# Sixty-four tokens by row instead of fifty-six, selected first with a row for each token and head, in the expert layer of a hybrid decoder step

## The chip, the cores and the metric

One core of one Trainium2 chip runs the whole program. The metric is the device time of one execution in microseconds (us); the time before is 2587.82 us, the median of three runs (2585.52 to 2590.06).

## The reference, cut to what matters

The program is one decoder layer for 264 tokens (256 of a prompt and 8 samples) of width 2048 in float32. The change touches one part of it, the PEER expert layer: each token gets 8 heads of queries, each query is scored against two sets of 128 keys, the 16 best of each set are combined to 256 candidates, and the 16 best candidates name 16 of 16384 experts. An expert is one row of `u_tab` and one row of `v_tab`.

```python
def peer(x, w_q, keys1, keys2, u_tab, v_tab):
    q = (xt @ w_q).reshape(n_pad, PEER_HEADS, 2, PEER_DKEY // 2)
    s1 = jnp.einsum('thd,hkd->thk', q[:, :, 0], keys1)
    s2 = jnp.einsum('thd,hkd->thk', q[:, :, 1], keys2)
    t1, i1 = lax.top_k(s1, PEER_TOPK)
    t2, i2 = lax.top_k(s2, PEER_TOPK)
    cand = (t1[..., :, None] + t2[..., None, :]).reshape(n_pad, PEER_HEADS, PEER_TOPK * PEER_TOPK)
    cand_idx = (i1[..., :, None] * PEER_KEYS + i2[..., None, :]).reshape(...)
    top, pos = lax.top_k(cand, PEER_TOPK)
    idx = jnp.take_along_axis(cand_idx, pos, axis=-1)
    gate = jax.nn.softmax(top, axis=-1)
    hid = jax.nn.gelu(jnp.einsum('td,thkd->thk', xb, u_tab[ib]), approximate=False)
    coef = gb * hid
    return jnp.einsum('thk,thkd->td', coef, v_tab[ib])
```

## The kernel before, in words

**Precision.** Every dense product is split: a weight tile of 128 x 1024 is loaded from DRAM by the SP queue (L142), ScalarE casts it to its high part (L153) and VectorE subtracts to get the low part (L154). Such a tile is half of a block of 128 output columns, a "half-block". Five tiles can wait for the split and four, later five, can be split ahead of the matmuls.

**The experts, two ways.** For most tokens (`TD = T - NSP`, 208 before) all 16384 experts are computed densely. In the U stage, 128 blocks (`pair_block`, L263) multiply x1 by the whole of `u_tab`; the activations go to DRAM (`a_d`). Meanwhile `gates` builds for each token a 128 x 128 map of its gates from one-hot operands (three of four on POOL, the fourth on VectorE, the others on ScalarE, a matmul each) and writes it to DRAM (`g_d`). In the V stage, 8 times 16 blocks multiply activations times gates (`prep`, L1408) by `v_tab` and add into `acc` (L1454). A block has 16 matmuls over 2 x TD columns (L273, L276: the weights' high part against both parts of the tokens) and 16 over TD columns (L274: the low part).

For the last `NSP` tokens (56 before: 48 of the prompt and the 8 samples) the experts' rows are gathered instead (`sparse_experts`, L1261). A gather of 128 rows of 8 KB by row numbers in `sidx` (L1269, on POOL's queue) fills a tile `ug`, and VectorE either multiplies and sums it against the tokens' own x1 (L1339, for `u`) or adds it times a coefficient to `x1s` (L1347, L1349, for `v`). The tokens come in groups of 32, 16 and 8 (`GR`); at a group's end matmuls with `fld` fold the 128 rows back to the tokens (L1310). A gathered tile needs 1 MB; there are 56 for `u` and 56 for `v`.

**The selection.** The scores of all tokens are computed head by head during the query product before U (`head_topk`, L1074): two tiles of 128 tokens with a column for each head, and one in which the 8 samples have a row for each sample and head. `topk` takes five VectorE operations for 16 of 128. `select` (L1110) then works in the U stage, on the second 128 tokens, the samples, and the first 128 tokens, in that order: 16 of 112 candidates per head, then a lookup of the two key numbers in three passes over 16 x 16 (compare with an iota, multiply, sum: L1161, L1164, L1166). `send` (L1210) writes row numbers and gates of the rowwise tokens to DRAM, and `index` (L1273) loads them back with a row for each token and slot. Three transposes (L1196) bring the selection of the dense tokens to `slot`, from which `gates` reads.

**The order.** It is written out by the program. After each half-block `tick(budget)` lets background tasks issue instructions: each task says after a piece how much VectorE time it thinks to have used (`yield 1.1`), or that it waits some half-blocks (`yield ("w", 2)`). The budget of a half-block is 1.1 in U and V. A gathered tile is due each 3.5 half-blocks until `to_v` and each 3.75 after it (L1336); `gates` puts four tokens in each 3 half-blocks. V can start when the gates are done ("G0") and `prep(0)` has run. On every engine the instructions run in the order in which they were issued.

Of the kernel before, what the change touches and what calls it, by code (L numbers as in the profile page):

```python
# [17 lines left out]
D = 2048  # L18
# [4 lines left out]
NSP = 56  # L23
# [24 lines left out]
GR = ((0, 32), (32, 16), (48, 8))  # L48
# [3 lines left out]
def hybrid_step(ctx: ExitStack, tc: tile.TileContext, xT, pT, w_in, w_dt, w_bs, w_bc, w_o, w_q, w_pg, w_pp,  # L52
# [64 lines left out]
    fld = cpool.tile([128, NSP], F, name="fld")  # L117
    x1sp = cpool.tile([128, KB, NSP], F, name="x1sp")
    sidx = cpool.tile([128, NSP], U32, name="sidx")
    scf = cpool.tile([128, NSP], F, name="scf")  # L120
    shid = cpool.tile([128, NSP], F, name="shid")
# [906 lines left out]
    keys_sb = {}  # L1028
    Q = {}

    TT = ((PT // 2, 128, PH), (PT, 64, 1), (0, 128, PH))
# [8 lines left out]
    TV = [[t1.tile([128, nh, TOPK], F, name=f"tv{t}{s}") for s in range(2)] for t, (_, _, nh) in enumerate(TT)]  # L1040
    TI = [[t1.tile([128, nh, TOPK], U32, name=f"ti{t}{s}") for s in range(2)] for t, (_, _, nh) in enumerate(TT)]
    zq = t2.tile([128, 2, PH, 64], F, name="zq")
    gp.memset(zq, 0.0)
    SC, P = {}, {}
# [4 lines left out]
    def load_keys(h):  # L1049
        k = t2.tile([128, 2, 128], F, name="keys", tag="keys", bufs=2)  # L1050
        gp.dma_start(out=k, in_=keysT[:, 2 * h:2 * h + 2, :])
        keys_sb[h] = k

    def q_evac(j):
        def f(ps):
            def late():
                t, sb = n1.product(ps)
                soon(lambda: ac.activation(t, t, AF.Identity, bias=sb))
                Q[j] = t
                if j % 2 == 1:  # L1060
                    spawn(head_topk(j // 2))

            defer(3, late)
        return f

    def topk(v, a, i, n):
        ve.max(a[:, 0:8], v)
        ve.max_index(i[:, 0:8], a[:, 0:8], v)
        w = t2.tile([128, 128], F, name="sw", tag="sw", bufs=2)
# [4 lines left out]
    def head_topk(h):  # L1074
        load_keys(h)
        yield ("w", 2)
        for s in range(2):
            ac.copy(zq[:, s, h, 8 * h:8 * h + 8], Q[2 * h + s][:, PT:T])
        yield ("w", 1)
        k = keys_sb.pop(h)  # L1080
        ps2 = {}
        for t in (0, 2):
            t0, n, _ = TT[t]
            ps = bank("scr")
            for s in range(2):
                te.matmul(ps[:n, s * 128:(s + 1) * 128], Q[2 * h + s][:, t0:t0 + n], k[:, s], start=True, stop=True)
            v = t2.tile([128, 2, 128], F, name="sv", tag="sv", bufs=3)
            ac.copy(v[:n].rearrange("p s k -> p (s k)"), ps[:n, 0:256])  # L1088
            ps2[t] = v
            yield 0.1  # L1090
        if h == 0:
            SC["ps"] = bank("scp")
        for s in range(2):
            te.matmul(SC["ps"][:64, s * 128:(s + 1) * 128], zq[:, s, h], k[:, s],
                      start=(h == 0 and s == 0), stop=(h == PH - 1), skip_group_check=True)
        if h == PH - 1:
            v = t2.tile([128, 2, 128], F, name="sv", tag="sv", bufs=3)
            ac.copy(v[:64].rearrange("p s k -> p (s k)"), SC.pop("ps")[:64, 0:256])
            ps2[1] = v
        for t, v in sorted(ps2.items()):  # L1100
            n = TT[t][1]
            for s in range(2):
                hh = h if t != 1 else 0
                topk(v[:n, s], TV[t][s][:n, hh], TI[t][s][:n, hh], n)
                yield 1.1
        Q.pop(2 * h)
        Q.pop(2 * h + 1)
        DONE[h] = True

    def select(t, sel):  # L1110

        _, n, nh = TT[t]
        sp = P["sp"]
        w = nh * TOPK
        top = sp.tile([128, nh, TOPK], F, name="top", tag="top", bufs=1)
        pos_u = sp.tile([128, nh, TOPK], U32, name="posu", tag="posu", bufs=1)

        cand = sp.tile([128, nh, 112], F, name="cand", tag="cand", bufs=1)
        v1, v2 = TV[t][0][:n], TV[t][1][:n]
        ve.tensor_tensor(cand[:n, :, 0:64].rearrange("p h (a b) -> p h a b", b=16),  # L1120
                         v1[:, :, 0:4, None].to_broadcast([n, nh, 4, 16]),
                         v2[:, :, None, :].to_broadcast([n, nh, 4, 16]), OP.add)
        ve.tensor_tensor(cand[:n, :, 64:112].rearrange("p h (a b) -> p h a b", b=4),
                         v1[:, :, 4:16, None].to_broadcast([n, nh, 12, 4]),
                         v2[:, :, None, 0:4].to_broadcast([n, nh, 12, 4]), OP.add)
        yield 1.1
        for h in range(nh):
            cf = cand[:n, h]
            a, i = top[:n, h], pos_u[:n, h]
            ve.max(a[:, 0:8], cf)  # L1130
            ve.max_index(i[:, 0:8], a[:, 0:8], cf)
            ve.match_replace(cf, a[:, 0:8], cf, NEG)
            ve.max(a[:, 8:16], cf)
            ve.max_index(i[:, 8:16], a[:, 8:16], cf)
            yield 0.95
        pu = pos_u[:n].rearrange("p h k -> p (h k)")
        ab_f = sp.tile([128, 4, w], F, name="abf", tag="abf", bufs=1)
        sh = sp.tile([128, w], U32, name="sh", tag="sh", bufs=2)
        ve.tensor_scalar(sh[:n], pu, 4, None, OP.logical_shift_right)
        ve.tensor_copy(ab_f[:n, 2], sh[:n])  # L1140
        sh = sp.tile([128, w], U32, name="sh", tag="sh", bufs=2)
        ve.tensor_scalar(sh[:n], pu, 2, None, OP.logical_shift_right)
        ve.tensor_copy(ab_f[:n, 3], sh[:n])
        fa, fb = ab_f[:n, 0], ab_f[:n, 1]
        ve.scalar_tensor_tensor(fa, ab_f[:n, 3], -12.0, ab_f[:n, 2], OP.add, OP.max)
        ve.tensor_scalar(ab_f[:n, 2], fa, 4.0, 48.0, OP.mult, OP.add)
        ve.scalar_tensor_tensor(ab_f[:n, 2], fa, 16.0, ab_f[:n, 2], OP.mult, OP.min)
        ve.tensor_copy(fb, pu)
        ve.tensor_tensor(fb, fb, ab_f[:n, 2], OP.subtract)
        yield 1.4  # L1150
        HH = max(1, nh // 4)
        for s in range(2):
            af = ab_f[:, s].rearrange("p (h k) -> p h k", h=nh)
            idf = sp.tile([128, nh, TOPK], F, name="idf", tag="idf", bufs=1)
            ve.tensor_copy(idf[:n], TI[t][s][:n])
            sv = sel[:n, s].rearrange("p (h k) -> p h k", h=nh)
            for h0_ in range(0, nh, HH):
                hs = slice(h0_, h0_ + HH)
                big = sp.tile([128, HH, TOPK, TOPK], F, name="big", tag="big", bufs=1)
                sh4 = [n, HH, TOPK, TOPK]  # L1160
                ve.tensor_tensor(big[:n], af[:n, hs, :, None].to_broadcast(sh4),  # L1161
                                 iot[:n, None, None, 0:TOPK].to_broadcast(sh4), OP.is_equal)
                yield 0.6 if nh > 1 else 0.4
                ve.tensor_tensor(big[:n], big[:n], idf[:n, hs, None, :].to_broadcast(sh4), OP.mult)  # L1164
                yield 0.6 if nh > 1 else 0.4
                ve.tensor_reduce(sv[:, hs], big[:n], AX.X, OP.add)  # L1166
                yield 0.6 if nh > 1 else 0.4
        gt = sel[:n, 2].rearrange("p (h k) -> p h k", h=nh)
        ve.tensor_tensor(gt, top[:n], top[:n, :, 0:1].to_broadcast([n, nh, TOPK]), OP.subtract)
        yield ("w", 1)  # L1170
        ac.activation(gt, gt, AF.Exp)
        sm = sp.tile([128, nh], F, name="sm", tag="sm", bufs=2)
        ve.tensor_reduce(sm[:n], gt, AX.X, OP.add)
        ve.reciprocal(sm[:n], sm[:n])
        ve.tensor_tensor(gt, gt, sm[:n, :, None].to_broadcast([n, nh, TOPK]), OP.mult)
        yield 0.8

    def select_all():
        while sum(h in DONE for h in range(PH)) < PH:
            yield ("w", 1)  # L1180
        t2_stack.close()
        sp = P["sp"] = sp_stack.enter_context(tc.tile_pool(name="select", bufs=1))
        P["oh"] = oh_stack.enter_context(tc.tile_pool(name="onehot", bufs=1))
        for t, (t0, n, nh) in enumerate(TT):
            sel = sp.tile([128, 3, nh * TOPK], F, name=f"sel{t}")
            yield from select(t, sel)
            if t < 2:
                send(sel, t, nh)
            if t == 1:
                spawn(sparse_experts(), True)  # L1190
            if t != 1:
                nd = min(n, TD - t0)
                yield ("w", 2)
                ps = bank("slt")
                for q in range(3):
                    te.transpose(ps[:, q * 128:q * 128 + n], sel[:n, q], ident[:n, :n])  # L1196
                for q in range(3):
                    ac.copy(slot[q][:, t0:t0 + nd], ps[:, q * 128:q * 128 + nd])
                if t == 0:
# [467 lines left out]
```

## Time and profile before

| | |
|---|---|
| three runs | 2585.52, 2587.82, 2590.06 us |
| the profiled execution | 2587.27 us, of which the span is 2585.5 us |
| granted TensorE clock, mean | 0.998 |
| bytes moved by DMA | 689.02 MB, mean 266 GB/s |
| the query product with the key scores | about 1020 to 1142 us |
| U stage | 1142.1 to 1829.9 us |
| V stage | 1829.9 to 2466 us |

A profile shows one execution. PE is TensorE, PEld its weight loads, DVE VectorE, ACT ScalarE, POOL GpSimd, SP the queue that loads weights. The recorded length of a matmul includes its way through the array, and neighbours overlap, so the distance between two starts tells what a matmul costs. A share of busy time is a mean over the whole span.

### The profile page before, as it was taken

What the parts mean: (1) busy time and instruction counts of PE and PEld (TensorE: products, weight loads), DVE (VectorE), ACT (ScalarE), POOL (GpSimd) and SP (SyncE); (2) the same over time, 40 slices, a digit from 0 to 9 for tenths busy, and PEclk for the clock granted to TensorE, in tenths of its full rate; (3) what the DMA queues carried; (4) which work ended last, traced back from release to release, by engine and by line L of the source; (5) the groups of instructions that cost most, each with busy time, mean ns of one, the idle gap of its engine ahead of it and who ended that gap; (6) DMA issues with size and microseconds to landing.
All of it is one profiled execution on the core that took longest, in us unless ns stands there. A gap on an engine that the chain in (4) does not pass through costs nothing.

```text
span 2585.5 us, 49226 instructions
## 1 busy us (share of the span) xinstructions
PE 2556.8 (99%) x19049; PEld 2532.4 (98%) x19049; DVE 2038.0 (79%) x3296; ACT 1433.7 (55%) x2206; POOL 620.6 (24%) x720
## 2 busy tenths in 40 slices
PE   9999999999999999999999999999999999999999
PEld 9999999999999999999999999999999999999999
DVE  7899965557445557889989777778889988889986
ACT  5665543445334444655578778866544454444563
POOL 2332200000000010100148567633332223222210
PEclk9999999999999999999999999999999999999999
DMA  6798765655665655567779999999999999999664
GB/s 229 228 292 282 244 184 168 183 175 181 180 184 178 183 179 180 172 186 221 220 243 365 363 357 357 356 364 376 375 362 377 371 364 356 375 358 366 206 196 123
DMA packets 202779, 689.02 MB, mean 266 GB/s; under 512 B 23040, under 2 KB 60464, under 8 KB 187312
## 3 DMA queue, kind: packets, MB, share of 16 engines
q1 hardware_dynamic: 154832, 495.49, 57.9%
q0 software_dynamic: 28688, 158.69, 16.1%
q10 hardware_dynamic: 19024, 31.69, 3.3%
q8 instruction: 149, 2.44, 0.4%
q14 instruction: 86, 0.70, 0.1%
HBM read 646.32 MB, written 39.46 MB: 265 GB/s over the span
## 4 chain that ended last, share of the span: by engine, by line
PE 72%; DVE 14%; DMA 9%; issue 3%; ACT 2%; ACTq 0%; POOL 0%; SPq 0%; DVEq 0%; POOLq 0%
PE mm L273 17%; PE mm L239 14%; PE mm L237 14%; PE mm L238 14%; PE mm L274 9%; DVE wlo L154 6%; DMA w<-vP 5%; DMA w<-uT 2%; PE gps L1258 1%; ACT whi L153 1%; PE mm L276 1%; DVE ug L1339 1%; DMA w<-w_in 1%; DVE as L1384 1%; DVE x1s L1349 1%
## 5 line engine op out<-in xcount | busy, mean ns | idle before, releaser
L154 DVE TENSOR_TENSOR wlo<-w,whi 128x1024 fp32r<-128x1024 f32 x916 | 1114.5, 1223 | 412.3 <-ACT whi L153 409.6
L153 ACT CAST whi<-w 128x1024 fp32r<-128x1024 f32 x916 | 958.5, 1050 | 754.3 <-PE mm L238 283.9
L273 PE MATMUL mm<-x,whi 128*128 128x416 f32 x1920 | 593.0, 370 | 0.0
L273 PE MATMUL mm<-co,whi 128*128 128x416 f32 x1920 | 586.6, 367 | 0.0
L239 PE MATMUL mm<-x,wlo 128*128 128x264 f32 x1920 | 547.9, 285 | 4.1 <-DVE wlo L154 4.0
L237 PE MATMUL mm<-x,whi 128*128 128x264 f32 x1920 | 546.8, 285 | 0.0
L238 PE MATMUL mm<-x,whi 128*128 128x264 f32 x1920 | 544.8, 284 | 0.0
L274 PE MATMUL mm<-x,wlo 128*128 128x208 f32 x2048 | 510.6, 259 | 5.7 <-DVE wlo L154 5.2
L274 PE MATMUL mm<-co,wlo 128*128 128x208 f32 x2048 | 510.4, 259 | 2.8 <-DVE wlo L154 2.6
L274 PEld LDWEIGHTS mm<-x,wlo 128*128 128x128 f32 x2048 | 391.1, 191 | 9.9 <-DVE wlo L154 9.5
L274 PEld LDWEIGHTS mm<-co,wlo 128*128 128x128 f32 x2048 | 390.3, 191 | 5.9 <-DVE wlo L154 5.6
L239 PEld LDWEIGHTS mm<-x,wlo 128*128 128x128 f32 x1920 | 360.8, 188 | 5.7 <-DVE wlo L154 5.6
L273 PEld LDWEIGHTS mm<-x,whi 128*128 128x128 f32 x1920 | 361.6, 188 | 3.5 <-ACT sv L1088 0.5
L273 PEld LDWEIGHTS mm<-co,whi 128*128 128x128 f32 x1920 | 360.7, 188 | 2.6
L237 PEld LDWEIGHTS mm<-x,whi 128*128 128x128 f32 x1920 | 361.6, 188 | 1.4 <-issue 1.4
L238 PEld LDWEIGHTS mm<-x,whi 128*128 128x128 f32 x1920 | 360.6, 188 | 0.0
L1245 POOL TENSOR_SCALAR o<-iot,slot,slot 128x128 f32<-128x128 f32 x156 | 200.4, 1291 | 3.3 <-issue 1.5
L1269 POOL DMA_INDIRECT ug<-vR,sidx x56 | 103.7, 1852 | 286.5 <-DVE x1s L1349 212.5
L1269 POOL DMA_INDIRECT ug<-uR,sidx x56 | 93.3, 1666 | 257.1 <-DVE ug L1339 199.9
L1339 DVE SCALAR_TENSOR_TENSOR ug<-ug,x1s 128x2048 f32<-128x2048 f32 x56 | 127.8, 2282 | 0.0
L1349 DVE SCALAR_TENSOR_TENSOR x1s<-ug,scf,x1s 128x2048 f32<-128x2048 f32 x53 | 124.2, 2344 | 0.0
L875 POOL CAST r1h<-r1gbh 128x2 fp32r<-128x2 f32 x16 | 4.5, 278 | 475.8 <-PE mm L239 475.8
(364 smaller groups left out, 3956.0 us busy)
## 6 DMA issues: line engine op xcount, KB each, us to landing
w<-uT SPq DMA_DIRECT2D x256, 512.0 KB
w<-vP SPq DMA_DIRECT2D x256, 512.0 KB
w<-w_in SPq DMA_DIRECT2D x240, 512.0 KB
w<-w_bc SPq DMA_DIRECT2D x32, 512.0 KB
w<-w_bs SPq DMA_DIRECT2D x32, 512.0 KB
w<-w_o SPq DMA_DIRECT2D x32, 512.0 KB
w<-w_q SPq DMA_DIRECT2D x32, 512.0 KB
w<-w_pg SPq DMA_DIRECT2D x32, 512.0 KB
```

Of the source, the lines that this page charges most:

```text
L153: ac.copy(hi, w)
L154: ve.tensor_tensor(lo, w, hi.bitcast(F), OP.subtract)
L237: te.matmul(ps, wh, xh[kb], start=(first and q == 0), stop=False)
L238: te.matmul(ps, wh, xl[kb], start=False, stop=False)
L239: te.matmul(ps, wl, xh[kb], start=False, stop=(last and q == n - 1))
L273: te.matmul(ps, hi[:, ws], xp[kb], start=(kb == 0), stop=False)
L274: te.matmul(ps[:, :TD], lo[:, ws], xp[kb][:, :TD], start=False, stop=False)
L276: te.matmul(ps, hi[:, ws], xp[kb], start=False, stop=True)
L1245: (gp if q < 3 else ve).tensor_scalar(o1[:, q], iot, slot[0][:, c], slot[2][:, c], OP.is_equal, OP.mult)
L1269: gp.indirect_dma_start(out=t, out_offset=None, in_=tab, in_offset=bass.IndirectOffsetOnAxis(ap=sidx[:, c:c + 1], axis=0))
L1339: ve.scalar_tensor_tensor(t, t, 1.0, x1s, OP.mult, OP.mult, accum_out=shid[:, c:c + 1])
L1349: ve.scalar_tensor_tensor(x1s, t, scf[:, c:c + 1], x1s, OP.mult, OP.add)
```

## The change

The number of rowwise tokens goes from 56 to 64, in four groups of 16 (`GT`, `NG`), so a group's 128 rows are 16 tokens x 8 heads, and the dense tokens from 208 to 200. The key scores of the tokens from 128 on are written to DRAM (`sc_d`) as soon as a head is done, and come back as tiles with a row for each token and head (`row_select`); nine such tiles (`RG`) hold the 64 rowwise tokens (four) and the 72 dense tokens from 128 to 199 (five, two of which overlap). The first 128 tokens keep a column for each head (`dense_topk`). The first rowwise group is selected first, then the first 128 tokens, then the 72 dense ones, whose result goes to DRAM (`sl_d`) and comes back by token, then the other rowwise groups. The row numbers of a rowwise group are written straight into `sidx`. The lookup subtracts 256 x position from 256 x iota + key number and takes the smallest absolute value: two passes. Budgets and cadences change with it. The diff, cut to its core:

```diff
-NSP = 56
+NSP = 64
-GR = ((0, 32), (32, 16), (48, 8))
+GT = 16
+NG = NSP // GT
+PA = 128
+RG = tuple(range(TD, T, GT)) + tuple(min(k, TD - GT) for k in range(PA, TD, GT))
...
+    def row_scores(h):
+        k = load_keys(h, "kr")
+        yield ("w", 2)
+        ps = bank("scr")
+        scores(ps, h, PA, 128, k, 0)
+        scores(ps, h, PA + 128, T - PA - 128, k, 256)
...
+        gp.dma_start(out=sc_d[0:128, h], in_=v)
+        gp.dma_start(out=sc_d[128:T - PA, h], in_=w[:T - PA - 128])
+        DONE["r" + str(h)] = True
+        if h == PH - 1:
+            spawn(sparse_first(), True)
+            spawn(replicate(0), True)
...
+    def row_select(g0, g1):
...
+            gp.dma_start(out=sv[g].rearrange("p s k -> p (s k)"), in_=sc_d[k:k + GT].rearrange("i h d -> (i h) d"))
...
+            for s in range(2):
+                topk(v[:, s], RV[s][:, g], RI[s][:, g], 128)
+                yield 1.5
...
+        yield from select([x[:, g0:g1] for x in RV], [x[:, g0:g1] for x in RI], nh, sel)
...
+    def sparse_rows(g0, g1):
+        yield from row_select(g0, g1)
...
+        ve.scalar_tensor_tensor(fx, sel[:, 0], 128.0, sel[:, 1], OP.mult, OP.add)
+        ve.tensor_copy(sidx[:, ks], fx)
+        ve.tensor_copy(scf[:, ks], sel[:, 2])
...
+    def sparse_first():
+        while "sp" not in P:
+            yield ("w", 1)
+        yield from sparse_rows(0, 1)
+        DONE["row0"] = True
+        spawn(sparse_experts(), True)
...
-                ve.tensor_tensor(big[:n], af[:n, hs, :, None].to_broadcast(sh4),
-                                 iot[:n, None, None, 0:TOPK].to_broadcast(sh4), OP.is_equal)
-                ve.tensor_tensor(big[:n], big[:n], idf[:n, hs, None, :].to_broadcast(sh4), OP.mult)
-                ve.tensor_reduce(sv[:, hs], big[:n], AX.X, OP.add)
+                ve.tensor_tensor(big, idf[:, hs, None, :].to_broadcast(sh4),
+                                 af[:, hs, :, None].to_broadcast(sh4), OP.subtract)
+                ve.tensor_reduce(sv[:, hs], big, AX.X, OP.min, apply_absolute_value=True)
...
     def select_all():
+        while "topk" not in DONE:
+            yield ("w", 1)
...
+        yield from select(TV, TI, PH, sel)
+        yield ("w", 2)
+        slots(sel, 0, PA)
+        DONE["sel0"] = True
+        tasks.insert(0, {"gen": all_gates(), "wait": clock["t"] + 1})
...
+        yield from row_select(NG, len(RG))
+        rs = P.pop("sel")
+        for g in range(NG, len(RG)):
+            k = RG[g] - PA
+            gp.dma_start(out=sl_d[:, k:k + GT, :].rearrange("q i (h k) -> (i h) q k", k=TOPK),
+                         in_=rs[:, :, (g - NG) * TOPK:(g - NG + 1) * TOPK])
+        yield ("w", 2)
+        sel = sp.tile([128, 3, PH * TOPK], F, name="sel", tag="sel", bufs=1)
+        gp.dma_start(out=sel[:TD - PA], in_=sl_d.rearrange("q t s -> t q s"))
+        yield ("w", 2)
+        slots(sel, PA, TD - PA)
+        DONE["sel1"] = True
+        for g0, g1 in ((1, 2), (2, NG)):
+            yield from sparse_rows(g0, g1)
+            DONE["row" + str(g0)] = True
...
-            yield grid(STEP - (i % (4 if vp else 2) == 0))
+            yield grid((STEP - (i % 3 == 0)) if "V" in DONE else (STEP - (i % 3 > 0)) if "sel0" in DONE else 5)
...
-                yield 2.4
+                yield 2.25
...
-        pair_block(x1_p, u_evac(e), 1.1)
-        if nxt is None and "G0" in DONE and not later:
+        pair_block(x1_p, u_evac(e), 1.25 if "sel0" in DONE else 1.1)
+        if nxt is None and "G" in DONE and not later:
             nxt = to_v()
```

## Rows read from the trace of the kernel before

**Rows 1.** The page, part 1: busy time of each engine (share of the span).
```profile
PE 2556.8 (99%) x19049; PEld 2532.4 (98%) x19049; DVE 2038.0 (79%) x3296; ACT 1433.7 (55%) x2206; POOL 620.6 (24%) x720
```

**Rows 2.** Windows of U and V: length, busy time (instructions), clock, DMA share, GB/s.
```profile
1142.10:1829.90 687.80, 679.45 (x4611) 670.62 (x4610) 580.81 (x987) 496.71 (x833) 308.93 (x239) 1.00 0.89 321
1829.90:2466.00 636.10, 632.28 (x4220) 626.14 (x4219) 575.45 (x627) 310.79 (x370) 179.51 (x185) 1.00 0.94 348
```

**Rows 3.** Timeline of PE: start, length, engine, line, operation, count.
```profile
1303.11 1.07 PE L1258 MATMUL gps<-o,o 128*128 128x128 f32 x8
1303.93 0.44 PE L273 MATMUL mm<-x,whi 128*128 128x416 f32 x1
...
1951.17 0.37 PE L273 MATMUL mm<-co,whi 128*128 128x416 f32 x1
1951.38 0.26 PE L274 MATMUL mm<-co,wlo 128*128 128x208 f32 x1
...
1955.39 0.97 PE L1310 MATMUL yS<-fld,x1s 128*128 128x32 f32 x8
1956.20 0.44 PE L273 MATMUL mm<-co,whi 128*128 128x416 f32 x1
```

**Rows 4.** Windows of single stretches, columns as in rows 2.
```profile
700.00:725.00 25.00, 25.00 (x208) 25.00 (x208) 11.38 (x12) 9.76 (x11) 0.00 (x0) 1.00 0.64 182
...
1275.00:1300.00 25.00, 22.92 (x142) 22.50 (x142) 23.45 (x55) 19.19 (x34) 8.16 (x10) 0.93 0.77 246
...
1375.00:1725.00 350.00, 349.46 (x2417) 347.64 (x2416) 275.79 (x325) 284.92 (x496) 234.01 (x168) 1.00 0.95 359
1725.00:1830.00 105.00, 101.76 (x668) 98.85 (x667) 86.18 (x85) 62.16 (x91) 30.74 (x26) 1.00 0.99 381
1830.00:2380.00 550.00, 547.25 (x3646) 541.68 (x3645) 494.10 (x503) 264.03 (x292) 159.05 (x140) 1.00 0.97 367
...
2000.00:2025.00 25.00, 25.00 (x167) 24.84 (x167) 21.85 (x24) 12.09 (x13) 5.57 (x5) 1.00 1.02 395
```

**Rows 5.** Groups by line (and form) on DVE: count, busy us, mean ns, idle before.
```profile
L154 DVE TENSOR_TENSOR wlo<-w,whi 128x1024 fp32r<-128x1024 f32 x916 | 1114.5, 1223 | 412.3 <-ACT whi L153 409.6
L1339 DVE SCALAR_TENSOR_TENSOR ug<-ug,x1s 128x2048 f32<-128x2048 f32 x56 | 127.8, 2282 | 0.0
...
L1384 DVE TENSOR_TENSOR as<-mm,as 128x208 f32<-128x208 f32 x128 | 47.0, 367 | 0.0
...
L1161 DVE TENSOR_TENSOR big<-abf,iot 128x512 f32<-128x512 f32 x8 | 5.5, 687 | 0.1
L1166 DVE TENSOR_REDUCE sel<-big 128x32 f32<-128x512 f32 x8 | 5.4, 681 | 0.1
...
L1161 DVE TENSOR_TENSOR big<-abf,iot 64x256 f32<-64x256 f32 x2 | 0.8, 410 | 0.0
```

**Rows 6.** Instructions on the gathered tiles in V: count, ns min/median/max, first and last start.
```profile
L1349 DVE SCALAR_TENSOR_TENSOR x1s<-ug,scf,x1s x34: 2340/2344/2352, 1829.8 to 2407.6; 128x2048 f32<-128x2048 f32 x34
L1269 POOL DMA_INDIRECT ug<-vR,sidx x34: 935/1724/2862, 1832.4 to 2386.7; - x34
L1269 POOL DMA_INDIRECT ug<-uR,sidx x24: 1677/1722/1946, 1934.5 to 2309.2; - x24
```

**Rows 7.** Waits in V: who for whom, us in total, times, longest.
```profile
ACT whi L153 <- DMA w<-vP: 211.3, 139, 4.8
...
PE mm L274 <- DVE wlo L154: 2.6, 5, 1.2
```

**Rows 8.** Timeline of POOL around the first gather.
```profile
1308.74 0.60 POOL L1275 DMA_DIRECT2D sidx<-sx_d  x1
...
1312.01 1.05 POOL L1269 DMA_INDIRECT ug<-uR,sidx  x1 [2.12 <-DMA sidx<-sx_d]
```

**Rows 9.** Timeline of PE at the transposes of the second tokens' selection.
```profile
1284.54 0.33 PE L1196 MATMUL slt<-ident,sel 128*128 128x128 f32 x1 [2.08 <-DVE sel L1175]
...
1285.02 0.59 PE L273 MATMUL mm<-x,whi 128*128 128x416 f32 x1
...
1285.58 0.59 PE L273 MATMUL mm<-x,whi 128*128 128x416 f32 x1
```

More of the change, by code (lines that the diff above doesn't have):

```diff
@@ new lines, in dense_topk @@
+    def dense_topk():
+        keys = {0: load_keys(0, "kd")}
+        old = None
+        yield ("w", 2)
+        for h in range(PH + 1):
+            new = None
+            if h < PH:
+                while "r" + str(h) not in DONE:
+                    yield ("w", 1)
+                k = keys.pop(h)
+                ps = bank("scr")
+                scores(ps, h, 0, PA, k, 0)
+                new = t2.tile([128, 2, 128], F, name="sv", tag="sv", bufs=2)
+                ac.copy(new.rearrange("p s k -> p (s k)"), ps[:, 0:256])
+                Q.pop(2 * h)
+                Q.pop(2 * h + 1)
+                if h + 1 < PH:
+                    keys[h + 1] = load_keys(h + 1, "kd")
+            if old is None:
+                yield ("w", 1)
+            else:
+                for s in range(2):
+                    topk(old[:, s], TV[s][:, h - 1], TI[s][:, h - 1], 128)
+                    yield 1.5
+            old = new
+        DONE["topk"] = True
@@ L1113, in select @@
+    def select(tv, ti, nh, sel):
         sp = P["sp"]
         w = nh * TOPK
[L1115 to L1144, printed above, removed]
@@ L1178, in select_all @@
     def select_all():
-        while sum(h in DONE for h in range(PH)) < PH:
+        while "topk" not in DONE:
             yield ("w", 1)
         t2_stack.close()
-        sp = P["sp"] = sp_stack.enter_context(tc.tile_pool(name="select", bufs=1))
+        sp = P["sp"]
         P["oh"] = oh_stack.enter_context(tc.tile_pool(name="onehot", bufs=1))
[L1184 to L1199, printed above, removed]
-                    tasks.insert(0, {"gen": gates(t0, nd), "wait": clock["t"] + 1})
@@ new lines, in select_all, with all_gates @@
+        yield ("w", 2)
+        sel = sp.tile([128, 3, PH * TOPK], F, name="sel", tag="sel", bufs=1)
+        gp.dma_start(out=sel[:TD - PA], in_=sl_d.rearrange("q t s -> t q s"))
[5 more added lines that the diff above has]
+            DONE["row" + str(g0)] = True
+    def all_gates():
+        yield from gates(0, PA)
+        while "sel1" not in DONE:
+            yield ("w", 1)
+        yield ("w", 1)
+        yield from gates(PA, TD - PA)
+        DONE["G"] = True
@@ L1507, in hybrid_step @@
         tick(1.2)
-        if "G0" in DONE and not later:
+        if "G" in DONE and not later:
             nxt = to_v()
```

284 lines of the change are left out of this document (143 added, 141 removed).

## The prediction

> **What bounds the kernel now.** I read the engine line of the page first: TensorE is busy for 99% of the span, VectorE for 79% [rows 1]. So the first question is what one matmul costs, not what an engine waits for. The change touches the two expert stages alone: the dense first product (the U stage, 1142.1 to 1829.9 us) and the dense second product (the V stage, to 2466 us). The windows by stage give them 687.8 and 636.1 us, with VectorE busy for 581 and 575 us and the DMA engines for 0.89 and 0.94 [rows 2]. In both, 128 blocks of 16 pairs of matmuls run, one of 416 columns (weights' high part, both halves of the tokens) and one of 208 (low part).
>
> What a pair costs is in the start times: a 416-column matmul starts at 1951.17 and its partner 0.21 us later [rows 3]; the 25 us window at 2000 holds 167 matmuls, so a pair takes 0.2994 us and the partner the other 0.09 [rows 4]. 2048 pairs are 613 us a stage. The rest of a stage is small: the gate matmuls (two records for each of 208 tokens; eight take 1303.11 to 1303.93 [rows 3], 0.1025 us each, so 43 us for 416), the folds, transposes and scores (about 13 us in U, 12 in V at the same price). That leaves some 18 us of stalls in U and 11 in V. The granted clock is 1.00 in nearly all of it [rows 4].
>
> Behind TensorE three suppliers run almost level with it. In V from 1830 to 2380 VectorE is busy 494 of 550 us and the DMA share is 0.97 at 367 GB/s [rows 4]; ScalarE's cast of a weight tile waited last for that tile's DMA 139 times in the 256 half-blocks, 211 us in all, but TensorE waited for the low-part split only 2.6 us [rows 7]. So the supply in V is paced by DMA and is just fast enough.
>
> **The change part by part.** All is summed against the profiled execution's 2587.27 us (span 2585.5 and 1.8 around it); the median shown, 2587.82, lies 0.55 above it.
>
> *Fewer dense columns.* 64 rowwise tokens leave 200 dense ones: 400 and 200 columns in place of 416 and 208, in 4096 pairs. What do eight columns in the partner buy? Eight fold matmuls with only 32 columns take 1955.39 to 1956.20, 0.101 us each, as long as eight with 128 columns [rows 3]: a full weight tile has a floor of about 0.10 to 0.11 us whatever streams past it. 208 columns at the 2.4 GHz level stream in 0.087 us, below that floor; 200 stay below it. The 264-column stage shows 25 us / 208 = 0.120 us [rows 4], which is 264/2.4 + 0.010, so above the floor columns count. 0.11 (floor) + 416/2.4 + 0.01 = 0.293 to 0.300 fits the pair; columns alone (624/2.4 + 0.02 = 0.280) do not. I therefore let only the long matmul gain: 16/2.4 = 6.67 ns, times 4096 = **-27.3 us**. The other end is all 24 columns, 10 ns, -41.0 us.
> The Trainium skill (TensorE: Matmul & The Clock Gate, Back-to-back issue gap) gives an isolated gap of N/2.4 + 2.5 ns; by it a pair would take 265 ns and all 24 columns would count. The trace's 300 ns speaks against it; it is kept as a rival.
>
> *Small TensorE work.* Eight fewer tokens: 16 gate records at 0.1025, -1.6 us. Four groups of 16 tokens in place of 32, 16 and 8: 128 fold records for 96 (+3.2 us) and 64 transposes for 48 (+1.6 us). The score matmuls stay the same in number (12 records a head); they only move earlier into the query stage. Together +3.2. So TensorE's own work falls by 27.3 - 3.2 = **24.1 us**, about 13 in U and 11 in V.
>
> *VectorE.* 128 gathered tiles in place of 112: 16 times 2.28 or 2.34 us [rows 5, 6] = +37 us. The lookup loses the third pass: before, 48 operations of 512 elements and 6 of 256, 0.685 and 0.41 us = 35 us; after, 20 and 28 = 25 us, if a subtract costs what the compare costs and a minimum of absolute values what the sum costs (the nearest rows, 0.687 and 0.681 [rows 5]; the bounds are half and double, -12 and +25 us). Five selections for three add about 10 us of short operations. Top-k counts are the same (34 of 128 columns, 17 of 112). VectorE's sum rises by some 37. It lies beside TensorE: by the code's cadence, a gather each 3.5 half-blocks in U and 3.75 in V becomes each 5 until the first selection is done, then 3.33, then 3.67 in V. The rowwise selection comes first, so gathers start some 45 half-blocks earlier than the 1312 us of now [rows 8], into a stretch with DMA to spare. I count 63 gathered tiles in U (now 112 - 58 = 54) and 65 in V (now 58 [rows 6]). U then has VectorE at about 604 of 674 us, V at 588 of 623: 90% and 94%, now 84% and 90%. A cover is there, thinner: I charge its loss below.
>
> *DMA.* +16.8 MB of gathers. In V one half-block moves 0.524 MB of weights, 0.10 of gates and activations and 1.05/3.67 of gathers, 0.91 MB; at TensorE's new pace (2.33 us, 2.38 with folds and transposes) that is 382 GB/s, now 372 at its pace and 367 measured. The V window at 2000 moved 395 GB/s without a stall, the end of U (1725 to 1830) 381 with 3 us of them [rows 4]. So V gets near its wall but not clearly past it: I charge **+4 us** there, bounds 0 (395 holds) and +11 (the supply keeps today's pace and V gains nothing). At the end of U, where gates are done but the gathers are denser, demand is 0.99 MB per 2.33 us, over 400 GB/s: **+2**, bounds 0 and +5.
>
> *The round trips through DRAM.* The selection's row numbers are now read in place, so the six small writes and six small loads of now go, with the 2.1 us for which the first gather waited [rows 8]; worth 0 to -2 us, I take 0. In their place the scores of tokens 128 and up go to DRAM and come back by token and head, off TensorE's way. One trip lies on TensorE's queue: the 72 dense tokens of the second half are selected by row, written to DRAM in five DMAs with 64-byte pieces, loaded back and transposed. The code allows 4 half-blocks, 10.5 us. Five issues at 0.55, a landing of 3.3 (1308.74 to 1312.01 [rows 8]), another issue and landing: 10 us on a quiet DMA, and there it is busy. Waiting on GpSimd: the gates' one-hot operations and the next gather; on TensorE: all dense matmuls behind the transposes. Today's transposes show the price of being late: 2.1 us of idle, after which pairs start 0.56 us apart (1285.02 to 1285.58) [rows 9], in a 25 us window whose granted clock is 0.93 [rows 4], so for a few us at the 1.2 GHz level. I take **+4 us**, bounds 0 and +12.
>
> *Tail.* The last gathered tile is consumed at 2407.6 of V's 2466 [rows 6]. With the new cadence it comes about 7 half-blocks (17 us) later, but its chain (fold, reduce, 18 us) still ends about when the last dense block does: 0, bounds 0 and +6.
>
> Sum: 2587.3 - 24.1 + 4 + 2 + 4 = **2573**.
>
> **Rivals.**
> 1. *Nothing hides worse.* VectorE has 6% left in V and DMA has shown 395 GB/s. Then the charges vanish: 2563 us. For it: TensorE waited for splits only 2.6 us in V. Against: the 139 DMA waits.
> 2. *The supply keeps its pace.* If DMA is the true bound in V, a faster TensorE waits: V stays at 636, U gains 5 to 8 less the round trip: about 2583. For it: share 0.97 throughout. Against: 395 GB/s in single windows. The Trainium skill (DMA: Bandwidth & Descriptors, Specifications) puts HBM at about 358 GB/s a core; by that V would be at the wall already and come out so. The windows of 367 and 395 disagree with the figure.
> 3. *VectorE becomes the bound (slower).* Place: U from the first gather to the last rowwise selection, where gathers, selection and weight splits share VectorE in order. A half-block there has 1.22 of split, 0.18 of evacuation (half of 0.367) [rows 5], a gather's 2.34/3.33 = 0.70 and a budget of 1.25 of which 0.55 is left for selection: 2.65 us, and TensorE's half-block with gates is 2.33 + 0.28 = 2.61. If short operations cost a tenth more than budgeted and gathers land late, each of some 120 half-blocks gives 0.2 us away (24 us), with the V charge of 11: 2598. It decides once VectorE needs over 2.8 us a half-block. Against: VectorE's short operations overlap a little, and its busy share at 1375 to 1725 is only 276 of 350 [rows 4].
> 4. *All columns count:* a further -14: 2559 with my charges, 2549 without.
> That the change does not do what it says I rule out: the shapes fix the columns.
>
> **How the numbers follow.** Forecast 0.45 (2566 to 2581), rival 1 0.18, rival 2 0.20, rival 3 0.12, rival 4 0.05. About 0.2% (5 us) is what a measurement of this kernel can tell from no change, so faster means under 2582.6 and slower over 2593. Faster: 0.45 + 0.18 + 0.05 and a little of rival 2, 0.70; same: the rest of rival 2 and the mild end of rival 3, 0.17; slower 0.13. The range that leaves out the strong ends of rivals 3 and 4 is 2558 to 2593.
>
> **What would show it.** Right: 0.293 us a pair in the V windows (170 matmuls in 25 us), the partner still 0.10 behind; U near 676 us, V near 629; VectorE 94% in V; a stall of a few us with the clock below 1.00 where the second transposes of the selection stand. Wrong: a pair at 0.29 or below (rival 4), a pair of 0.293 but V unchanged with more waits of the cast for DMA (rival 2), or waits of TensorE for the split of tens of us in U (rival 3).

## The result, and the profile after

The changed kernel takes 2603.66 us (median of six runs, 2598.85 to 2605.21); the kernel before, run beside it, 2588.94 (median of six). The ratio is 1.0057, 95% interval 1.0043 to 1.0071: slower by 15 us, where 2573 was forecast. One of the six runs before took 8306 us and is unlike all others; the median of the other five is 2587.82. The profiled execution took 2604.17 us.

Page, part 1, of the changed kernel (compare [rows 1]):

```profile
PE 2542.5 (98%) x19081; PEld 2520.6 (97%) x19081; DVE 2066.5 (79%) x3372; ACT 1430.8 (55%) x2172; POOL 659.2 (25%) x756
```

TensorE lost 14 us of busy time (24.1 were forecast), yet the span grew by 17. So the time is in waits. The windows of U, of V and of three single stretches (columns as in [rows 2]; compare [rows 2, 4]) say where:

```profile
1147.10:1839.10 692.00, 664.98 (x4601) 661.19 (x4601) 599.85 (x1044) 495.00 (x824) 334.31 (x248) 0.98 0.91 334
1839.10:2474.00 634.90, 623.88 (x4213) 616.84 (x4211) 579.23 (x627) 305.23 (x334) 185.56 (x194) 0.99 0.95 357
1500.00:1525.00 25.00, 9.95 (x58) 9.69 (x58) 10.69 (x12) 9.76 (x18) 12.93 (x15) 0.66 0.76 266
2000.00:2025.00 25.00, 24.86 (x174) 24.58 (x173) 20.13 (x21) 15.59 (x20) 7.81 (x8) 1.00 1.01 391
2475.00:2500.00 25.00, 15.54 (x100) 15.24 (x101) 16.93 (x37) 14.10 (x35) 0.81 (x4) 0.73 0.43 131
```

U grew by 4 us instead of shrinking by 12; V is as long as before; and two windows at 1500 and 2475 hold 58 and 100 matmuls where a full one holds over 170, at granted clocks of 0.66 and 0.73. By the start times, the query stage ahead of U takes 108.1 us (101.5 before), U 692.0 (688.0), V 634.8 (635.1), all behind V's last matmul 128.5 (120.2).

The price of a pair is as forecast. The timeline of PE in V (compare [rows 3]):

```profile
2249.65 0.36 PE L277 MATMUL mm<-co,whi 128*128 128x400 f32 x1
2249.85 0.26 PE L278 MATMUL mm<-co,wlo 128*128 128x200 f32 x1
2249.94 0.36 PE L277 MATMUL mm<-co,whi 128*128 128x400 f32 x1
...
2251.99 0.36 PE L277 MATMUL mm<-co,whi 128*128 128x400 f32 x1
```

Eight pairs start in 2.34 us, 0.2925 each, where 0.2994 was measured before; the low partner costs 0.09, as far as two digits show. The gain is there in each undisturbed pair and is lost in waits.

**V.** The waits in V, 1850 to 2380 us (who for whom, us in total, times, longest; compare [rows 7]), and then those of SP's queue alone:

```profile
ACT whi L157 <- DMA w<-vP: 238.5, 165, 5.9
...
DVE wlo L158 <- ACT whi L157: 45.0, 45, 2.9
...
PEld mm L278 <- DVE wlo L158: 10.1, 17, 1.6
```

```profile
SPq L146 <- DVE wlo L158: 419.8, 211, 4.2
```

ScalarE's cast waits for the weights in 165 of 215 half-blocks. But look at SP, which issues their loads: 211 times it waited for the split on VectorE. The load of a weight tile goes out the moment a buffer comes free, and all five buffers are always in use. In the records of these 215 tiles (161 of them have a landing) a buffer is held, on the mean, 8.06 us from issue to landing, 0.13 until the cast starts, 1.05 for the cast, 1.70 in VectorE's queue, 1.22 for the split, and 0.03 until the next load is issued: 12.2 us. Five buffers then give a tile each 2.44 us (530 us for 215 tiles is 2.465), and TensorE would take one each 2.34 (eight pairs), some 2.38 with folds and transposes. I read V as a loop of five buffers, at whose end TensorE waits: its loads of the low part wait 10.1 us for the split. The experiments test this reading.

**U.** The timeline of GpSimd, and then of PE, at the selection's round trip through DRAM (compare [rows 9]):

```profile
1497.04 3.15 POOL L1268 DMA_DIRECT2D sl_d<-rsel  x4
1506.46 0.76 POOL L1268 DMA_DIRECT2D sl_d<-rsel  x1 [6.27 <-DMA sl_d<-rsel]
1507.27 3.70 POOL L1304 TENSOR_SCALAR o<-iot,slot,slot 128x128 f32<-128x128 f32 x3
1511.14 1.08 POOL L1347 DMA_INDIRECT ug<-vR,sidx  x1 [0.17 <-issue]
1512.22 0.81 POOL L1272 DMA_DIRECT2D sel<-sl_d  x1
```

```profile
1517.48 0.62 PE L1246 MATMUL slt<-ident,sel 72*128 72x72 f32 x3 [15.05 <-DMA sel<-sl_d]
1517.85 0.68 PE L277 MATMUL mm<-x,whi 128*128 128x400 f32 x1
...
1518.49 0.58 PE L277 MATMUL mm<-x,whi 128*128 128x400 f32 x1
...
1519.04 0.58 PE L277 MATMUL mm<-x,whi 128*128 128x400 f32 x1
```

Four writes go out from 1497.04; the fifth waits 6.27 us for the landing of an earlier one, because the last two groups of 16 tokens overlap by eight and write the same rows of DRAM. Behind it in the queue stand three one-hot operations and a gather; the read is issued at 1512.22 and lands after 1517. TensorE, in whose queue the transposes stand, stops for 15.05 us, and its next pairs start 0.55 us apart, at the 1.2 GHz level.
The Trainium skill (DMA: Bandwidth & Descriptors, "Anatomy of one DMA — SWDGE (gpsimd) path") says that a transfer's fixed cost is mostly the receipt of its last write, and that this can be long when the target is HBM. The trace shows the whole alone: these five writes of 24 KB landed 3.3 to 8.4 us after their issue; what part of it is the receipt, no run here shows.

**Tail.** The timeline of PE behind the last dense matmul, and then of ScalarE:

```profile
2473.82 0.36 PE L280 MATMUL mm<-co,whi 128*128 128x400 f32 x1
2481.83 0.59 PE L1579 MATMUL mm<-pp,whi 128*128 128x264 f32 x1 [7.65 <-ACT pp L1530]
2485.05 0.59 PE L1580 MATMUL mm<-pp,whi 128*128 128x264 f32 x1 [2.64 <-DVE pp L1531]
```

```profile
2478.30 1.29 ACT L930 ACTIVATE r<-x1sp,cpar 128x64 fp32r<-128x64 f32 x5
...
2480.43 0.82 ACT L930 ACTIVATE r<-x1sp,cpar 128x64 fp32r<-128x64 f32 x3
2481.16 0.61 ACT L1530 CAST pp<-pi 128x528 fp32r<-128x528 f32 x1
```

The projection waits 7.65 us for its input `pp`, whose cast stands on ScalarE behind the copies of the second normalization (L930), and 2.64 more for the low part. Instructions on the gathered tiles in V (compare [rows 6]) show why this is later than before:

```profile
L1394 DVE SCALAR_TENSOR_TENSOR x1s<-ug,scf,x1s x32: 2340/2344/2349, 1839.4 to 2445.6; 128x2048 f32<-128x2048 f32 x32
L1347 POOL DMA_INDIRECT ug<-uR,sidx x32: 994/1720/2810, 1842.0 to 2277.1; - x32
...
L1347 POOL DMA_INDIRECT ug<-vR,sidx x32: 977/1715/2875, 1989.8 to 2428.6; - x32
```

The last gathered tile is consumed at 2445.6, 28 us before V's last matmul at 2473.8; before it was 2407.6, 58 us ahead of 2465.2.

### The profile page after: what moved, and what is told of

It is laid out like the page before. It is cut to its first block, busy times and chain, and to the rows that moved or that the text cites. A ratio compares the mean times of both kernels' runs of the same rounds, so it can differ in the third digit from the quotient of the medians.

```text
span 2602.3 us, 49365 instructions
## 1 busy us (share of the span) xinstructions
PE 2542.5 (98%) x19081; PEld 2520.6 (97%) x19081; DVE 2066.5 (79%) x3372; ACT 1430.8 (55%) x2172; POOL 659.2 (25%) x756
## 3 DMA queue, kind: packets, MB, share of 16 engines
q8 instruction: 149, 2.44, 0.4%
## 4 chain that ended last, share of the span: by engine, by line
PE 69%; DMA 12%; DVE 11%; issue 5%; ACT 2%; POOL 1%; ACTq 0%; DVEq 0%; SPq 0%; POOLq 0%
PE mm L241 14%; PE mm L243 14%; PE mm L242 14%; PE mm L277 14%; DMA w<-vP 7%; PE mm L278 7%; DVE wlo L158 5%; DMA ug<-vR,sidx 2%; PE gps L1317 1%; DMA w<-uT 1%; ACT whi L157 1%; DVE acc L1501 1%; DVE x1s L1394 1%; POOL o L1304 1%; PE mm L280 1%
## 5 line engine op out<-in xcount | busy, mean ns | idle before, releaser
L277 PE MATMUL mm<-x,whi 128*128 128x400 f32 x1920 | 582.4, 367 | 1.8 <-ACT whi L157 1.8
L277 PE MATMUL mm<-co,whi 128*128 128x400 f32 x1920 | 576.5, 364 | 0.8 <-ACT whi L157 0.8
L278 PE MATMUL mm<-x,wlo 128*128 128x200 f32 x2048 | 506.6, 258 | 9.0 <-DVE wlo L158 8.8
L278 PE MATMUL mm<-co,wlo 128*128 128x200 f32 x2048 | 508.1, 258 | 6.9 <-DVE wlo L158 6.7
L1304 POOL TENSOR_SCALAR o<-iot,slot,slot 128x128 f32<-128x128 f32 x150 | 211.7, 1419 | 25.0 <-issue 11.9
L1347 POOL DMA_INDIRECT ug<-uR,sidx x64 | 105.6, 1650 | 352.5 <-DVE ug L1384 272.6
L1347 POOL DMA_INDIRECT ug<-vR,sidx x64 | 110.2, 1722 | 312.8 <-DVE x1s L1394 199.2
L1384 DVE SCALAR_TENSOR_TENSOR ug<-ug,x1s 128x2048 f32<-128x2048 f32 x64 | 146.6, 2291 | 3.7 <-DMA ug<-uR,sidx 3.7
L1394 DVE SCALAR_TENSOR_TENSOR x1s<-ug,scf,x1s 128x2048 f32<-128x2048 f32 x60 | 140.7, 2345 | 2.9 <-DMA ug<-vR,sidx 2.9
```

The source lines that it names most:

```text
L277: te.matmul(ps, hi[:, ws], xp[kb], start=(kb == 0), stop=False)
L278: te.matmul(ps[:, :TD], lo[:, ws], xp[kb][:, :TD], start=False, stop=False)
L1304: (gp if q < 3 else ve).tensor_scalar(o1[:, q], iot, slot[0][:, c], slot[2][:, c], OP.is_equal, OP.mult)
L1347: gp.indirect_dma_start(out=t, out_offset=None, in_=tab, in_offset=bass.IndirectOffsetOnAxis(ap=sidx[:, c:c + 1], axis=0))
L1384: ve.scalar_tensor_tensor(t, t, 1.0, x1s, OP.mult, OP.mult, accum_out=shid[:, c:c + 1])
L1394: ve.scalar_tensor_tensor(x1s, t, scf[:, c:c + 1], x1s, OP.mult, OP.add)
```

## The experiments

All times are medians beside runs of the kernel before on the same chip; U, V and tail are read from the profiled execution, from the first 400-column matmul (416 in the kernel before) of each stage on.

| kernel | us | ratio to before, 95% interval | U | V | tail |
|---|---|---|---|---|---|
| before | 2588.94 | 1 | 688.0 | 635.1 | 120.2 |
| changed | 2603.66 | 1.0057, 1.0043 to 1.0071 | 692.0 | 634.8 | 128.5 |
| e1_late | 2595.98 | 1.0027, 1.0014 to 1.0041 | 683.2 | 634.2 | 125.8 |
| e2_nooverlap | 2601.14 | 1.0043, 1.0028 to 1.0058 | 693.2 | 640.2 | 125.9 |
| e3_nogather | 2587.51 | 0.9995, 0.9984 to 1.0006 | 691.7 | 618.1 | 126.1 |
| e4_short | 2583.58 | 0.9977, 0.9968 to 0.9986 | 691.7 | 615.6 | 125.6 |
| e5_pp | 2598.37 | 1.0034, 1.0022 to 1.0046 | 692.9 | 634.2 | 121.1 |
| e6_w6 | 2586.68 | 0.9990, 0.9981 to 0.9998 | 692.4 | 617.7 | 125.5 |
| e7_u | 2594.41 | 1.0023, 1.0013 to 1.0034 | 682.1 | 630.1 | 130.1 |
| e8_all | 2568.42 | 0.9914, 0.9902 to 0.9927 | 686.6 | 621.5 | 114.4 |
| e9_before_nogather | 2584.11 | 0.9986, 0.9977 to 0.9995 | 690.5 | 628.7 | 120.9 |
| e10_best | 2566.43 | 0.9914, 0.9901 to 0.9928 | 678.0 | 619.0 | 119.7 |

### What paces V: e3_nogather, e4_short, e6_w6, e9_before_nogather

First theory: the DMA engines' rate paces V; rival: VectorE's work does. e3_nogather and e4_short take one away each (e4_short narrows the product for `u` in the same way as the sum shown here).

```diff
# e3_nogather, in get(i)
-        rows = {}
+        rows, held = {}, {}
...
-                t = lp.tile([128, D], F, name="ug", tag="ug", bufs=2)
-                gp.indirect_dma_start(out=t, ...)
+                if "V" in DONE:
+                    t = held[i % 2]
+                else:
+                    t = lp.tile([128, D], F, name="ug", tag="ug", bufs=2)
+                    gp.indirect_dma_start(out=t, ...)
+                held[i % 2] = t
# e4_short
...
+                w = 128 if "V" in DONE else D
-                ve.scalar_tensor_tensor(x1s, t, scf[:, c:c + 1], x1s, OP.mult, OP.add)
+                ve.scalar_tensor_tensor(x1s[:, :w], t[:, :w], scf[:, c:c + 1], x1s[:, :w], OP.mult, OP.add)
```

> The changed kernel, where the gathers of second-expert rows in V are left out and VectorE computes on the two tiles that it holds; all VectorE work stays. Theory A (V is paced by the DMA supply of weights, which shares the engines with the gathers): V shrinks from 635 us by the narrower matmuls' share and what was lost to supply before, to 612-618 us, total about 2583. Rival B (VectorE is the bound in V): V stays at 633-636 us and the total at 2600-2604.

> The changed kernel, where in V VectorE's two operations on every gathered tile are 128 columns wide instead of 2048; the gathers all stay. Theory A (supply of weights by DMA paces V): V stays near 632-635 us, or even loses as gathers come in tighter bursts, total 2598-2604; the tail may gain some us as the sparse part ends earlier. Rival B (VectorE is the bound in V): V loses 15 to 25 us, total about 2580.

Both edits shorten V, from 634.8 us to 618.1 and 615.6. Windows of 1850 to 2380 us, the changed kernel, then e3_nogather and e4_short:

```profile
1850.00:2380.00 530.00, 523.85 (x3547) 517.82 (x3547) 480.08 (x501) 251.86 (x254) 155.90 (x136) 1.00 0.98 372
```

```profile
1850.00:2380.00 530.00, 530.00 (x3632) 529.94 (x3631) 499.76 (x515) 259.56 (x261) 50.06 (x80) 1.00 0.83 267
```

```profile
1850.00:2380.00 530.00, 530.00 (x3632) 529.94 (x3632) 391.27 (x514) 257.50 (x261) 130.09 (x140) 1.00 1.00 384
```

Without the gathers (267 GB/s for the changed kernel's 372) V is short with VectorE at 500 of 530 us, so VectorE is not the bound. With VectorE's load down to 391 us V is short while the DMA engines move 384 GB/s, so DMA's rate is not the bound either. My theory fell here, and its rival with it: e4_short, for which I had expected no gain, gave 19 us of V. What both edits shorten is the loop: e3_nogather its landing leg (5.0 us on the mean, by the updates of the loads' semaphores) and the 1.70 us in VectorE's queue (0.88 left), e4_short that queue alone (0.29 left). That made a third theory, and e6_w6 tests it without taking any work away.

```diff
 # fetch; the sixth buffer lives in V's pool
+            st["turn"] = (st["turn"] + 1) % (NW + 1)
+            if "vp" in st and st["turn"] == 0:
+                w = st["vp"].tile([128, 1024], F, name="w", tag="w", bufs=1)
+            else:
                 w = wpool.tile([128, 1024], F, name="w", tag="w", bufs=NW)
 # next_half
-        fetch(i + NW - 1)
+        fetch(i + NW - 1 + ("vp" in st))
...
```

> The changed kernel with a sixth buffer for weight tiles in the V stage (and one scratch block less of 13, to make room for it). Theory L (a loop: with five buffers, each in use from its load's issue to the end of its split, 12.2 us on the mean, V cannot take a tile more often than each 12.2/5 = 2.45 us, whatever TensorE needs): V falls from 635 us to TensorE's own pace, 616 to 619, and the whole to about 2586. Theory A (the DMA engines are at their rate): the weights only land later by one tile's time, V stays at 632 to 635 and the total at 2601 to 2604. Rival B (VectorE is the bound in V): the same as A, with VectorE's busy share unchanged.

V fell to 617.7, inside the 616 to 619, and the whole to 2586.68. Window, then waits, of 1850 to 2380 us:

```profile
1850.00:2380.00 530.00, 530.00 (x3635) 529.93 (x3634) 495.35 (x514) 258.93 (x261) 157.44 (x137) 1.00 1.00 383
```

```profile
ACT whi L161 <- DMA w<-vP: 111.4, 78, 2.9
ACT whi L161 <- PE mm L284: 72.6, 57, 2.2
ACT whi L161 <- PE mm L281: 62.0, 54, 2.1
```

And the wait of SP's queue alone:

```profile
SPq L150 <- DVE wlo L162: 429.4, 220, 6.5
```

All the bytes and all of VectorE's work are there, TensorE does not stop, and in 111 half-blocks the cast now waits for TensorE to give back a high-part buffer: the supply is ahead. So DMA's rate did not pace V. The sixth buffer alone makes the changed kernel as fast as the one before. (The scratch block given up for it cost nothing that the other stages show.)

Was V held by the loop before the change, too?

```diff
 # e9_before_nogather: the edit of e3_nogather, in the kernel before, where it also needs
+    DONE["V"] = True
```

> The kernel before (56 tokens by row), where the gathers in V are left out and VectorE computes on the two tiles that it holds. It tells how far the loop of five weight buffers already held V before the change. Theory L, with TensorE's pace of the kernel before (0.2995 us a pair, 2.40 us for eight pairs, 2.44 with folds and transposes) just under the loop's 2.45: V shrinks by no more than its stalls, 635 to 626-630 us, the total to 2579-2583; the changed kernel lost 17 us by the same edit. Rival (before the change V was as much held by supply as after it): V goes down by 15 us or more.

Windows of 1850 to 2380 us, the kernel before and then e9_before_nogather:

```profile
1850.00:2380.00 530.00, 527.25 (x3514) 521.80 (x3513) 479.83 (x490) 255.94 (x283) 152.92 (x135) 1.00 0.97 365
```

```profile
1850.00:2380.00 530.00, 530.00 (x3547) 527.29 (x3546) 487.36 (x494) 258.80 (x285) 52.07 (x82) 1.00 0.81 259
```

V falls by 6.4 us (the total, 2584.11, is 1 us above its range), where the same edit gave 16.7 after the change. With TensorE never idle in this stretch a half-block takes 530/218 = 2.43 us; with the gathers it took 530/216 = 2.454. Before the change the loop and TensorE ran within 1% of each other, and a faster TensorE could gain next to nothing.

One caution on the 12.2 us. As long as all buffers are in use, the time for which one is held is their number times the pace, whoever sets the pace: it is 12.2 us in e9_before_nogather, where TensorE never stops (five times 2.43), and 14.3 in e6_w6 (six times 2.38). SP waits for the split there too, 216 and 220 times. So neither the sum nor SP's wait tells who paces. What tells is the leg from the landing to the cast's start: 0.13 us in the changed kernel, 1.3 in e6_w6, 4.1 in e9_before_nogather. In the last two a landed tile often waits for its turn, and the cast waits for TensorE (111 and 170 times); in the changed kernel it does so 14 times.

### What U waits for: e1_late, e2_nooverlap, e7_u

```diff
# e1_late
-        yield ("w", 2)
-        slots(sel, PA, TD - PA)
-        DONE["sel1"] = True
+        def late_slots():
+            yield ("w", 10)
+            slots(sel, PA, TD - PA)
+            DONE["sel1"] = True
+        spawn(late_slots(), True)
# e2_nooverlap
+            lo = max(0, RG[g - 1] + GT - RG[g]) if g > NG else 0
-            gp.dma_start(out=sl_d[:, k:k + GT, :]..., in_=rs[:, ...])
+            gp.dma_start(out=sl_d[:, k + lo:k + GT, :]..., in_=rs[lo * PH:, ...])
```

> The changed kernel with one step moved: the transposes of the second tokens' slots, which read the selection back from DRAM, become a task of their own that waits ten weight tiles more, and the selection's task goes on with the row groups at once. Theory A (the round trip through DRAM is waited for by TensorE): the 15 us stop near 1502-1517 us and the half clock behind it go, some 17 us in all, about 2586 us; window 1500-1525 us shows over 165 matmuls at clock 1.00 where the changed kernel has 58. Rival B (VectorE is the bound, TensorE's stop only shows work that would have waited elsewhere): the stop moves to another place in U or into V and the time stays within 4 us of 2603.

> The changed kernel, where the fifth write of the selection to DRAM writes only the 8 tokens that the fourth has not written, so that it no longer waits for the fourth to land; everything else stays. Theory A: the 6.3 us that GpSimd's queue stands in front of the fifth write go, the read of the selection is issued 6 to 7 us earlier and TensorE's stop falls from 15 to some 9 us: about 2597 us. If the stop falls under what lets the clock drop, more, about 2590. Rival C (the wait is for the queue's other work, the gather and the one-hot operations, not for the overlap): the read is issued as late as before and the time stays at 2603.

e1_late gained 8 of 17. The waits from 1495 to 1525 us show that part of the stop only moved:

```profile
DVE rv L1070 <- DMA rsc<-sc_d: 8.7, 1, 8.7
...
POOL sl_d L1268 <- DMA sl_d<-rsel: 6.3, 1, 6.3
...
PE mm L278 <- DVE wlo L158: 2.6, 1, 2.6
```

The selection's task runs on to its next row group, and now VectorE stands 8.7 us for that group's scores, read back from DRAM behind the same write on GpSimd's queue; the weights' splits stand behind it.

In e2_nooverlap the wait for the overlap is gone and the time hardly moved: 2.5 us less than the changed kernel, with intervals that overlap (its profiled execution, 2608.1 us of span, is a longer one). Its waits from 1490 to 1525 us:

```profile
PE slt L1246 <- DMA sel<-sl_d: 11.9, 1, 11.9
...
POOL sel L1273 <- DMA sl_d<-rsel: 1.5, 1, 1.5
```

The five writes go out in one go, but TensorE still stops for 11.9 us: the round trip itself is too long for the time allowed. The time is rival C's, but its condition does not hold: the read goes out 10.8 us after the first write (1501.27 to 1512.08) where it took 15.2, and the stop is 3 us shorter. e7_u takes both edits and, behind each request for stored scores but that of the first group, waits eight weight tiles instead of three before VectorE uses them.

```diff
 # row_select
         get(g0)
-        yield ("w", 3)
+        yield ("w", 3 if g0 == 0 else 8)
```

> The changed kernel with all waits for the DRAM round trips in U moved away from the engines' queues: the transposes ten weight tiles later in a task of their own, the fifth write without overlap, and the first read of stored scores asked for five weight tiles earlier than VectorE uses it. If the round trips are what U loses, U goes from 692 us (683 with the first of the three alone) to 674 to 678, and the total to 2585 to 2590. If U's pace is set by VectorE or by supply, U stays at 683 or above and the total at 2595.

Missed: U 682.1, hardly better than e1_late alone. Its waits from 1505 to 1545 us name the next place:

```profile
POOL sel L1273 <- DMA sl_d<-rsel: 9.1, 1, 9.1
...
PE gps L1321 <- POOL o L1308: 7.1, 2, 6.2
```

The writes are now issued 17.7 us later (1514.72), the read waits 9.1 us for them at the head of GpSimd's queue, and the gates' one-hot operations behind it keep TensorE for 6.2. The same delay has been on TensorE's queue, on VectorE's and on GpSimd's.

### The tail: e5_pp

```diff
 # sparse_experts
             get(i + 1)
+            if i + 1 == len(jobs):
+                spawn(ple_parts())
 # finish
-        spawn(ple_parts())
```

> The changed kernel, where the last small input (its load, its cast and its low part, all before TensorE's projection) is prepared when the last gather has been issued instead of after the last fold of the gathered rows. Theory A (the stop of 8 us after the last dense block is the wait for this input, late because the gathers end later): the stop falls under 2 us and the half clock behind it goes, 2592 to 2597 us. Rival B (the whole chain of the second normalization is late, the input is only the first to wait): the stop comes back behind the projection and the time stays within 3 us of 2603.

The stop is 0.2 us, the tail 121.1: theory A, though its time, 2598.37, lies 1.4 us above the range. The second normalization was not what was late.

### Together: e8_all, e10_best

e8_all has the edits of e7_u, e5_pp and e6_w6. e10_best also takes the read off the head of GpSimd's queue:

```diff
-        yield ("w", 2)
-        sel = sp.tile(...)
-        gp.dma_start(out=sel[:TD - PA], in_=sl_d.rearrange("q t s -> t q s"))
         def late_slots():
-            yield ("w", 10)
+            yield ("w", 8)
+            sel = sp.tile(...)
+            gp.dma_start(out=sel[:TD - PA], in_=sl_d.rearrange("q t s -> t q s"))
+            yield ("w", 6)
...
```

> All of it together: the three moves in U, the early input of the projection and the sixth weight buffer in V. If the three losses are separate, their gains add: U 674 to 678, V 616 to 620, tail 120 to 122, about 2563 us in all. If one supply stands behind all three, the sum comes out smaller, 2575 or above.

> All five edits of the run before it and one more: the read of the written selection is issued eight weight tiles after the writes instead of two, so that GpSimd's queue does not stand in front of it (9.1 us there with the three moves in U, and TensorE behind it 6.2 us for the gates' one-hot tiles). Theory A: U falls from 686 us to 676-680, the total to 2559-2563. Rival (something else of that stretch is late next, VectorE's queue or the gathers): U stays above 683, the total at 2566-2570.

e8_all came out 5 us above the sum: U at 686.6 instead of 674 to 678, with the same wait for the one-hot operations as e7_u (6.1 us), and a tail 6 us shorter than expected: TensorE waits 0.3 us there, where it waits 4.1 for `acc` in e10_best and 3.9 in the kernel before; why it does not was not followed up. e10_best has U at 678.0, as theory A says, and beats both kernels, 2566.43 us, ratio 0.9914; its total misses theory A's 2559 to 2563 by 3 us and lies where the rival had it. The timed gain over e8_all is 2 us, not the 8.6 that U shows between the two profiled executions (2571.9 and 2565.7 us of span); the order of the two is not settled by their times. In the 25 us window that held 58 matmuls:

```profile
1500.00:1525.00 25.00, 24.14 (x171) 23.80 (x170) 20.58 (x24) 23.14 (x42) 18.60 (x13) 1.00 0.94 337
```

## Why the prediction was wrong, step by step

Against the forecast's stages (U 676, V 629, tail unchanged) the profiled execution is 16 us longer in U, 6 in V and 8 in the tail: 30 of the 31 us.

- *Fewer dense columns, -27.3: the amount right, the reason not, so in part luck.* 0.2994 to 0.2925 us a pair is -28 us over 4096 pairs, and rival 4 (all columns, -41) is out. But the long matmul alone was to gain, because the partner was held to lie on a floor of 0.10 to 0.11 us; the partner's 0.09 in the same rows already lay under it, and the sum with the floor gives 0.293, not up to 0.300. In V without gathers, where TensorE never stops (e9_before_nogather, e3_nogather; over 1600 pairs each), the mean distance from the long matmul to its partner falls from 205.3 to 200.6 ns and the one from the partner to the next long matmul from 96.3 to 93.5: 4.7 for 16 columns and 2.8 for eight. Both gained, neither in full.
- *Small TensorE work, +3.2: right as far as it shows.* The scores moved as said: 80 score matmuls in place of 36 lie in the query stage, 44 times the 0.1025 us of such a record are 4.5 of its +6.6 us.
- *VectorE, +37, beside TensorE: right in kind* (busy time +28.5; 91% of V, where 94 was foretold). Rival 3 foretold 2598, but its place is refuted: e10_best carries all of this work and has U at 678.
- *DMA in V, +4 (0 to +11): the step that failed in V.* I read the casts' waits for DMA as a rate and weighed 382 GB/s against a wall. The limit was the time for which a weight buffer is held over the number of buffers, 12.2 us over five. In the sum's terms the charge came out at its bound: V, at 634.8, kept all but 0.3 of its length, so the credit of 11 was lost. The sixth buffer gives back more, 634.8 - 617.7 = 17 us, because the loop had already cost the kernel before some 6 (e9_before_nogather). Rival 2 had V's length right (636) and the cause wrong, as I did: e6_w6 moved 383 GB/s over the same 530 us. No row that I had shown tells a rate from a loop: in the kernel before, too, SP waited for the split 210 times for 216 tiles, but so it does in e6_w6.
 The Trainium skill (HBM Reference, Specifications (TRN2)) gives a core's share as about 358 GB/s and some 425 for a core that streams alone. The runs fit the second better: 383 and 384 GB/s over 530 us.
- *DMA at the end of U, +2 (0 to +5): right as far as it shows.* From 1725 us to the end of U TensorE is idle for 7.5 of 114 us, before for 3.2 of 105 [rows 4]: some 4 us more.
- *The round trip, +4 (0 to +12): the step that failed in U.* The estimate was 10 us on a quiet DMA against 10.5 allowed; it took 20.4 (1497.04 to 1517.48). Missed were the write that waits for an overlapping one, three one-hot operations and a gather in the queue, and landings of up to 8.4 us under load. Its price, with the half clock behind it, is what e10_best gets back: 692.0 - 678.0 = 14 us.
- *Tail, 0 (0 to +6): failed, +8.3.* The last gathered tile was to come 17 us later; it came 38 later (9 of them because V starts later). The slack of the projection's input was never worked out; e5_pp shows that it was nearly all of the loss (128.5 to 121.1, before 120.2).

With the three waits taken away the same columns give 2566 us, near rival 1 (2563). This does not prove the credits right: the sixth buffer also took away some 6 us of waiting that the kernel before had, and rival 1 did not count on that; without them it would be about 2573, 10 above rival 1. Most of what is missing lies in U, 678 us where the forecast without its two charges (4 and 2) has 670: TensorE is idle there for 14 us in e10_best and for 8 before, 5.8 of the 14 in the last 102 us, at 403 GB/s. What paces that end was not tested.

## What to carry to other kernels

Before crediting a faster consumer, look at the loop that feeds it. That the loads' queue always waits for the release of a buffer says only that all buffers are in use. If, besides, tiles are taken up the moment they land and the consumer still waits, the pace may be the time for which a buffer is held, with every queue that it passes, over the number of buffers. One more buffer is the test that tells this from a DMA at its rate; here it gave 17 us, and a shorter landing or a shorter queue gave 17 and 19. A round trip through DRAM is to be allowed for at loaded landing times and with all that stands in each queue, and it must be waited for at no engine's head of queue: here, taken off one, it appeared on the next.

## What the runs showed of the hardware that was not expected

Weight tiles of 512 KB land after 7.7 us on the median with the gathers running (3.4 to 14.6, the 161 tiles of the changed kernel that have a landing) and after 4.6 without them (3.4 to 7.9, e9_before_nogather). A pair loses 7 ns with 24 columns fewer, where 24 columns at 2.4 GHz are 10. And a stop costs more than itself: after the 15.05 us in U and the 7.65 us in the tail TensorE's next matmuls ran at the 1.2 GHz level, 0.55 us a pair instead of 0.29 and 0.22 us a 264-column matmul instead of 0.12.
